# Deferring the opening group's element-wise tail behind the first head, and raising the priority of the meta products

## The chip, the cores and the metric

The kernel runs on one core of one Trainium2 chip. The metric is the device time of one execution in microseconds (us). The engines are PE (TensorE, matrix products), DVE (VectorE) and POOL (GpSimd) for element-wise work, ACT (ScalarE) for copies and activations, and SP (SyncE), which issues all DMAs from one queue in order. Each engine runs its own list of instructions strictly in order.

## The reference

One decoder layer on a sequence of 2048 rows with 16 learned meta rows put in front. The combined projection gives eight parts of 512 columns; four feed a gated short convolution, four a retention.

```python
hn = rms_norm(h, norm_g)
proj = jnp.einsum('bld,de->ble', hn, w_in)
cx, cb, cc, cg, q, k, v, rg = jnp.split(proj, N_PROJ, axis=-1)
conv_out = short_conv_branch(cx, cb, cc, conv_w) * jax.nn.silu(cg)   # cb * conv(cc * cx)
...
ret_out = ret.astype(h.dtype) * jax.nn.silu(rg)
mixed = jnp.concatenate([conv_out, ret_out], axis=-1)
return h + jnp.einsum('ble,ed->bld', mixed, w_out)
```

All of it is in float32. The retention works in chunks of 128 rows with a state per head; a final norm follows.

## The kernel before, in words

Every large product is made of three matmuls: each operand is split into a high part (`mh`, `wh`: a copy to the fp32r format on ACT) and a low part (`ml`, `wl`: source minus high part on DVE, L113), and high x low, low x high and high x high are summed in one PSUM bank. `split` (L98) does this.

The sequence is worked in two blocks of 1024 rows (r = 0, 1), each in two halves of 512 (j = 0, 1). In a block come eight units: four convolution groups and four retention heads. In block 0 the order is group 4 (the "opening group"), heads 0 to 3, then groups 5, 6 and 7 (`UNITS`, L36). Each unit has two "quads". A quad multiplies a 2 x 2 arrangement of weight blocks by a 2 x 2 arrangement of activation blocks. `quad` (L201) does this in seven products (a Winograd form) of 12 matmuls each; their operands are sums and differences of blocks. The weight sums are made in place on POOL by `stationary` (L123), from four raw tiles `ra` and a sum tile `sa`; their parts `wh`, `wl` have three buffers each. The third product needs a difference formed on POOL, its cast on ACT, its `wl` on DVE, and also the copy `tc` (L217) of the bank that the first product filled, since it goes on summing in that bank. `quad_plain` (L249) does the same quad without sums in eight products, 96 matmuls; the opening group uses it because the activation sums are not ready yet. The parts `ml` for two of the sums (`late_parts`, L791) take over buffers that the opening group's second quad still reads.

What each quad leaves in PSUM is taken over by a function `take`. For the opening group the first quad gives `u` (the product of two projections, copied by ACT and multiplied by DVE), which is multiplied by the row factors `rr2`, gets two columns in front by `carry` (L446, three small copies on POOL, the first two values coming from the meta rows through `meta_carry`, L424) and goes through three convolution taps, `taps` (L452: one on ACT, two on DVE for each half). The second quad gives for each half a gate and another factor: `take_plain` (L506) copies the bank to `cb` on ACT, multiplies the gate by `rr` on DVE, applies Silu on ACT, multiplies the tap result `c` by `rr` on POOL, and multiplies `c` by each of the two on DVE. `store_mixed` (L439) writes `c` to memory.

`meta_products` (L388) multiplies a unit's raw weight blocks by the 16 normalized meta rows: 16 small matmuls (32 passes on PE, plain float32) into one bank, then four small ACT copies to `mk`. `ahead` (L744) calls it for the next unit at the end of each unit. POOL may overwrite the raw blocks only after these matmuls.

The tile framework schedules all instructions by a priority, in essence the order in which the code writes them, and by its own estimate of when operands are ready; the resulting per-engine lists are fixed at build time. `tc.high_priority(offset=HIGH)` lets instructions be given out as if they were written 400 places earlier. `HIGH` is already defined in the kernel before (L30).

Of the kernel before, what the change touches and what calls it, by code (L numbers as in the profile page):

```python
# [14 lines left out]
P = 128  # L15
# [55 lines left out]
def hybrid_trunk(ctx: ExitStack, tc: tile.TileContext, t, out: bass.AP, chunk_decay):  # L71
# [20 lines left out]
    def gen(name="g"):  # L92
        return sb.tile([P, HB + 16], F32, name=name, tag="g", bufs=GEN)[:, : 2 + HB]
# [155 lines left out]
    def quad_plain(w, m, take, middle=None):  # L249

        for j in range(2):
            banks = [ps_proj() for _ in range(2)]
            for half in range(2):
                for kt in range(KH):
                    ks = slice(kt * P, (kt + 1) * P)
                    mh, ml = m[BLOCK[half][j]][kt]
                    for i in range(2):
                        wh, wl = w[2 * i + half]
                        for n, (a, b) in enumerate(((wl, mh), (wh, ml), (wh, mh))):
                            nc.tensor.matmul(  # L260
                                banks[i], a[:, ks], b, start=half + kt + n == 0,
                                stop=half == 1 and kt == KH - 1 and n == 2,
                            )
# [124 lines left out]
    def meta_products(blocks):  # L388

        bank = ps_misc()  # L390
        four = [bank[i * 32 : i * 32 + NMETA, :P] for i in range(4)]
        for kt in range(KH):
            for i in (3, 2, 1, 0):
                nc.tensor.matmul(  # L394
                    four[i], meta_s[:, i % 2 * KH + kt, :], blocks[i][:, kt * P : (kt + 1) * P],
                    start=kt == 0, stop=kt == KH - 1,
                )
        scratch = sb.tile([P, HB], F32, name="mk", tag="tc", bufs=COPIES).rearrange("p (a c) -> p a c", a=CH)
        for i in range(4):
            nc.scalar.copy(out=scratch[:NMETA, i], in_=four[i])  # L400
        return scratch
# [56 lines left out]
            )  # L458
        return c

    def conv_group(g, r, m, f, blocks, ahead, first=(), between=()):


        between = iter(between)
        u = [gen("u") for _ in range(2)]
        rr, rr2 = ([a[:, j * HB : (j + 1) * HB] for j in range(2)] for a in f[:2])
        held = [None]

        def mul(eng, out, a, b):
            eng.tensor_tensor(out=out, in0=a, in1=b, op=ALU.mult)  # L470

        def take(i, j, pp, c):
            s = u[j][:, 2:]
            if c is None:
                mul(nc.vector, s, pp, s)
            elif i == 1:
                add(nc.vector, c, pp, c)
                held[0] = c
            else:
                add(nc.vector, s, pp, c)  # L480
                mul(nc.vector, s, s, rr2[j])
                if j == 1:
                    mul(nc.gpsimd, s, s, held[0])

        def take_plain(i, j, pp, c):
            s = u[j][:, 2:]
            if i == 0:
                nc.scalar.copy(out=s, in_=pp)
            else:
                mul(nc.vector, s, pp, s)  # L490

        blocks, meta = blocks
        if len(first) > 0:
            quad_plain(first[0], m, take_plain)
        else:
            quad(stationary(blocks), m, take)
        next(between, lambda: None)()
        if len(first) > 0:
            for j in range(2):
                mul(nc.vector, u[j][:, 2:], u[j][:, 2:], rr2[j])  # L500
# [5 lines left out]
        def take_plain(i, j, pp, c):  # L506
            c = gen("cb")[:, :HB]
            nc.scalar.copy(out=c, in_=pp)
            if i == 0:
# [19 lines left out]
        if len(first) > 1:  # L529
            quad_plain(first[1], m, take_plain)  # L530
        else:
            quad(stationary(load_raw(w_loads(n))), m, take)
        next(between, lambda: None)()
        blocks = ahead()
        for j in range(2):
            store_mixed(r, j, g, cs[j])
        return blocks
# [216 lines left out]
    for r in range(NR):  # L754
        f = factors[r]
        rot_t = sb.tile([P, 2, BLK], F32, name="rot_t", tag="rot_t", bufs=1)
        p0 = NMETA + r * BLK

        def load_tables():
            nc.sync.dma_start(rot_t, t["rot"][:, :, p0 : p0 + BLK])  # L760

        if r == 0:
            w = [None] * 4
            loads = w_loads(2 * NG)

# [30 lines left out]
            between = (lambda: None, late_parts)  # L796
# [10 lines left out]
        units = UNITS[r]  # L807
        for n, unit in enumerate(units):
            following = units[n + 1] if n + 1 < len(units) else None
            rest = lambda: ahead(r, following)  # L810
            special = (first, between) if n == 0 else ()
            if unit < NG:
                blocks = head(unit, r, m, rot_t, f, blocks, rest, *special)
                if unit > 0:
                    next(later, None)
                    next(later, None)
            else:
                blocks = conv_group(unit - NG, r, m, f, blocks, rest, *special)
                if n > 0:
                    for _ in range(4 - r):  # L820
                        next(steps, None)

    m, b = moving(load_w_out)
    final_g = row_tile("final_g")
# [41 lines left out]
```

## Time and profile before

| | us |
|---|---|
| time, median of 3 runs (lowest, highest) | 907.0 (906.9, 907.28) |
| the profiled execution's own time | 906.71 |
| its span, first to last instruction | 904.9 |
| TensorE busy | 882.2 |
| VectorE busy | 717.7 |
| ScalarE busy | 407.7 |
| GpSimd busy | 392.2 |

A matmul's row in the timeline shows a duration of about 0.39 us, but successive matmuls overlap: the step from start to start is what it costs. "Idle before" in square brackets names what ended an engine's wait. All times in rows count from the span's start. Line numbers are those of the kernel before unless a sentence says otherwise.

### The profile page before, as it was taken

To read this page: it belongs to the slowest core of one execution; us is meant where nothing else is said; L and a number is where in the kernel's file an instruction comes from. 1 tells how busy PE (TensorE), PEld (TensorE's weight loads), DVE (VectorE), ACT (ScalarE), POOL (GpSimd) and SP (SyncE) were. 2 spreads that over 40 slices of the span, in tenths; PEclk is the share of its full clock that TensorE was granted. 3 is DMA by queue.
4 is the path that set the end of the run, shared out by engine and by line. 5 is a ranking of instruction groups with operands and counts; after the bars stand their busy time and mean duration, and the time that the engine had idled before them with its cause. 6 is when DMAs were issued, how large, how long until landed. Compare 5 with 4: busy or idle time off the path is not lost.

```text
span 904.9 us, 12864 instructions
## 1 busy us (share of the span) xinstructions
PE 882.2 (97%) x4407; PEld 726.5 (80%) x4407; DVE 717.7 (79%) x1176; ACT 407.7 (45%) x816; POOL 392.2 (43%) x291
## 2 busy tenths in 40 slices
PE   8988999999999999999999999999999999999996
PEld 5767788888888787788888888888887878788885
DVE  6897788898867966899889899777667697876664
ACT  8772433434244454655333332433333474555553
POOL 0552231313333565351333323345546444777773
PEclk9998999999999999999999999999999999999999
DMA  9712115436234252754125272113221685555532
GB/s 331 233 37 73 45 48 164 140 81 211 60 95 139 72 161 71 248 193 140 35 74 199 77 234 70 51 55 93 54 87 48 208 277 174 166 181 157 184 122 80
DMA packets 76242, 116.94 MB, mean 129 GB/s; under 512 B 7632, under 2 KB 24336, under 8 KB 76176
## 3 DMA queue, kind: packets, MB, share of 16 engines
q1 hardware_dynamic: 76176, 116.11, 39.9%
q8 instruction: 35, 0.57, 0.3%
q14 instruction: 31, 0.25, 0.1%
HBM read 90.92 MB, written 25.17 MB: 128 GB/s over the span
## 4 chain that ended last, share of the span: by engine, by line
PE 81%; DVE 8%; DMA 3%; ACT 3%; issue 2%; POOL 1%; SPq 0%; POOLq 0%; DVEq 0%; ACTq 0%
PE pj L210 67%; PE pj L260 5%; DVE ml L113 2%; DVE wl L113 2%; PE ms L642 1%; PE ms L619 1%; PE ms L643 1%; PE ms L632 1%; DMA ra<-in_x 1%; DMA x<-in_xT 1%; PE ms L394 1%; PE ms L604 1%; PE ms L609 1%; PE ms L666 1%; ACT mh L104 1%
## 5 line engine op out<-in xcount | busy, mean ns | idle before, releaser
L210 PE MATMUL pj<-mh,wl 128*128 128x512 f32 x1008 | 400.5, 397 | 9.6 <-DVE wl L113 7.0
L210 PE MATMUL pj<-ml,wh 128*128 128x512 f32 x1008 | 394.7, 392 | 1.1 <-DVE ml L113 1.1
L210 PE MATMUL pj<-mh,wh 128*128 128x512 f32 x1008 | 394.1, 391 | 0.0
L101 ACT CAST wh<-ra 128x512 fp32r<-128x512 f32 x216 | 133.9, 620 | 318.7 <-PE pj L210 275.8
L210 PEld LDWEIGHTS pj<-mh,wl 128*128 128x128 f32 x1008 | 189.9, 188 | 52.2 <-DVE wl L113 7.4
L113 DVE TENSOR_TENSOR wl<-ra,wh 128x512 fp32r<-128x512 f32 x216 | 194.0, 899 | 40.7 <-ACT wh L101 40.2
L210 PEld LDWEIGHTS pj<-mh,wh 128*128 128x128 f32 x1008 | 189.7, 188 | 39.8
L210 PEld LDWEIGHTS pj<-ml,wh 128*128 128x128 f32 x1008 | 190.1, 189 | 39.1 <-DVE ml L113 1.4
L113 POOL TENSOR_TENSOR ra<-ra 128x512 f32<-128x512 f32 x72 | 112.9, 1568 | 87.4 <-DVE qg L587 32.2
L110 POOL TENSOR_TENSOR sa<-ra 128x512 f32<-128x512 f32 x36 | 53.8, 1495 | 124.4 <-DVE wl L113 53.3
L113 POOL TENSOR_TENSOR ra<-sa,ra 128x512 f32<-128x512 f32 x36 | 51.2, 1423 | 92.4 <-DVE wl L113 88.9
L217 ACT COPY tc<-pj 128x512 f32<-128x512 f32 x108 | 62.6, 580 | 0.0
L260 PE MATMUL pj<-mh,ml 128*128 128x512 f32 x128 | 48.7, 397 | 2.2 <-DVE ml L113 1.7
L260 PE MATMUL pj<-ml,mh 128*128 128x512 f32 x128 | 50.3, 393 | 0.1
L260 PE MATMUL pj<-mh,mh 128*128 128x512 f32 x128 | 50.0, 393 | 0.0
L655 POOL TENSOR_TENSOR rp<-rs,neg_half 128x4 f32<-128x4 f32 x16 | 19.9, 1245 | 49.5 <-DVE rs L110 49.3
L470 POOL TENSOR_TENSOR c<-c,rr 128x512 f32<-128x512 f32 x16 | 29.6, 1852 | 25.3 <-DVE c L470 13.5
L696 DVE TENSOR_TENSOR yo<-pj,yo 128x512 f32<-128x512 f32 x32 | 22.0, 688 | 21.2 <-PE pj L210 11.4
L101 ACT CAST wh<-sa 128x512 fp32r<-128x512 f32 x36 | 22.4, 622 | 31.8 <-PE pj L210 31.6
L113 DVE TENSOR_TENSOR ml<-t,mh 128x512 fp32r<-128x512 f32 x40 | 35.6, 936 | 0.8 <-ACT mh L101 0.8
L659 DVE TENSOR_SCALAR pm<-ms,mv,rp 128x128 f32<-128x128 f32 x64 | 21.9, 405 | 15.8 <-POOL rp L655 15.8
L701 POOL TENSOR_TENSOR z<-yo,final_g 128x512 f32<-128x512 f32 x16 | 26.2, 1635 | 18.5 <-DVE yo L696 18.5
(132 smaller groups left out, 1129.2 us busy)
## 6 DMA issues: line engine op xcount, KB each, us to landing
ra<-in_w_in SPq DMA_DIRECT2D x128, 256.0 KB, 2.7
x<-in_xT SPq DMA_DIRECT2D x48, 256.0 KB, 5.0
w<-in_w_out SPq DMA_DIRECT2D x32, 256.0 KB, 5.1
ra<-mixed SPq DMA_DIRECT2D x32, 256.0 KB, 2.7
yo<-in_x SPq DMA_DIRECT2D x32, 256.0 KB, 4.1
ra<-in_x SPq DMA_DIRECT2D x16, 256.0 KB, 3.2
mixed<-c SPq DMA_DIRECT2D x16, 256.0 KB, 2.5
mixed<-qg SPq DMA_DIRECT2D x16, 256.0 KB, 2.3
```

The costliest lines, as they stand in the source:

```text
L101: nc.scalar.copy(out=hi, in_=src)
L104: nc.scalar.mul(hi, src, scale)
L110: eng.tensor_tensor(out=out, in0=a, in1=b, op=ALU.add)
L113: eng.tensor_tensor(out=out, in0=a, in1=b, op=ALU.subtract)
L210: nc.tensor.matmul(bank, a[:, ks], b, start=first and kt == 0 and n == 0, stop=kt == KH - 1 and n == 2, skip_group_check=not first,)
L217: nc.scalar.copy(out=c, in_=bank)
L260: nc.tensor.matmul(banks[i], a[:, ks], b, start=half + kt + n == 0, stop=half == 1 and kt == KH - 1 and n == 2,)
L470: eng.tensor_tensor(out=out, in0=a, in1=b, op=ALU.mult)
L655: nc.gpsimd.tensor_tensor(out=rp, in0=rs, in1=neg_half.rearrange("p (c a) -> p c a", a=1), op=ALU.pow)
L659: nc.vector.tensor_scalar(out=y[:, cs], in0=o[:, cs], scalar1=mv[:, c, 0:1], scalar2=rp[:, c, :], op0=ALU.subtract, op1=ALU.mult,)
L696: last[0] = nc.vector.tensor_tensor(out=y, in0=pp, in1=y, op=ALU.add)
L701: nc.gpsimd.tensor_tensor(out=ys[i][j], in0=y, in1=final_g[:, j * HB : (j + 1) * HB], op=ALU.mult)
```

## The change

`conv_group` loses its special path for the opening group, which gets a function of its own, `group_plain`. It issues both plain quads with takes that only copy: the first quad's `take` is as before, the second's copies all four banks to `cb` tiles and does nothing more. `meta_carry` stands between the quads. The rest (`u` times `rr2`, `carry`, taps, gates, multiplies, stores) is put in a closure, `complete`, which the first head calls between its two quads. `late_parts` and `ahead` keep their place at the end of the opening group. Second, the matmuls of `meta_products` are wrapped in `tc.high_priority`.

```diff
@@ meta_products
+        with tc.high_priority(offset=HIGH):
             for kt in range(KH):
                 for i in (3, 2, 1, 0):
                     nc.tensor.matmul(
                         four[i], meta_s[:, i % 2 * KH + kt, :], blocks[i][:, kt * P : (kt + 1) * P],
...
+    def group_plain(g, m, f, meta, first, between, ahead):
...
+        quad_plain(first[0], m, take)
+        meta_carry(g, meta)
+
+        def take(i, j, pp, c):
+            c = gen("cb")[:, :HB]
+            nc.scalar.copy(out=c, in_=pp)
+            raws.append(c)
+
+        quad_plain(first[1], m, take)
+        between()
+        blocks = ahead()
+
+        def complete():
+            for j in range(2):
+                mul(nc.vector, u[j][:, 2:], u[j][:, 2:], rr2[j])
+            carry(u, g, 0)
+            for j in range(2):
+                gate, other = raws[2 * j : 2 * j + 2]
+                c = taps(u[j], g)
+                mul(nc.vector, gate, gate, rr[j])
+                nc.scalar.activation(gate, gate, AF.Silu)
+                mul(nc.gpsimd, c, c, rr[j])
+                mul(nc.vector, c, c, gate)
+                mul(nc.vector, c, c, other)
+                store_mixed(0, j, g, c)
+
+        return blocks, complete
@@ conv_group
-        def take_plain(i, j, pp, c):
-            c = gen("cb")[:, :HB]
-            nc.scalar.copy(out=c, in_=pp)
-            if i == 0:
-                mul(nc.vector, c, c, rr[j])
-                nc.scalar.activation(c, c, AF.Silu)
-                mul(nc.gpsimd, cs[j], cs[j], rr[j])
-            mul(nc.vector, cs[j], cs[j], c)
@@ the loop over units
+            if r + n == 0:
+                blocks, complete = group_plain(unit - NG, m, f, blocks[1], first, late_parts, rest)
+                special = (), (complete,)
+            elif unit < NG:
+                blocks = head(unit, r, m, rot_t, f, blocks, rest, *(special if unit == 0 else ()))
```

What the scheduler makes of it is shown at three places. In the rows, `x2` or `x16` counts like instructions in a row.

The first place is the turn from the opening group to the first head, on DVE. The rows run from the carry copy (`carry<-ms`) to the `wl` of the first head's third product; `c`, `cb` and `u` belong to the opening group, `ml` to the activation sums, `mk` to the meta products. Before:

```order
L430 COPY carry_78<-ms 128x2
L456 SCALAR_TENSOR_TENSOR c<-u,conv_w,c 128x512
L470 TENSOR_TENSOR u<-u,rr_363 128x512
L456 SCALAR_TENSOR_TENSOR c<-u,conv_w,c 128x512 x2
L470 TENSOR_TENSOR cb<-cb,rr 128x512
...
L110 TENSOR_TENSOR mk<-mk 16x128
L470 TENSOR_TENSOR c<-c,cb 128x512 x3
L113 TENSOR_TENSOR wl<-ra,wh 128x512
```

And now (L431 is the carry copy there):

```order
L470 TENSOR_TENSOR cb<-cb,rr 128x512
...
L431 COPY carry_78<-ms 128x2
L470 TENSOR_TENSOR u<-u,rr_363 128x512
L110 TENSOR_TENSOR mk<-mk 16x128 x2
L470 TENSOR_TENSOR cb<-cb,rr 128x512
L113 TENSOR_TENSOR ml_672<-t_307,mh_671 128x512
L113 TENSOR_TENSOR wl<-ra,wh 128x512
```

All taps and all multiplies into `c` have left this stretch, and the gate's multiply of the first half has moved ahead of the carry copy. The same place on ACT, from the second half's row factors (`rr`, `rr_363`) to the copy `tc` of the head's first bank, before:

```order
L295 ACTIVATE rr_363<-ms 128x512
L454 ACTIVATE c<-u,conv_w 128x512
L508 COPY cb<-pj 128x512 x3
L101 CAST mh_694<-t_307 128x512
L508 COPY cb<-pj 128x512
...
L511 ACTIVATE cb<-cb 128x512
L217 COPY tc<-pj 128x512
L101 CAST wh<-ra 128x512
L101 CAST wh<-sa 128x512
```

And now:

```order
L295 ACTIVATE rr_363<-ms 128x512
L401 COPY mk<-ms 16x128 x4
L484 COPY cb<-pj 128x512
L101 CAST mh_671<-t_307 128x512
L101 CAST wh<-ra 128x512
L484 COPY cb<-pj 128x512
L101 CAST mh_679<-t_309 128x512
L499 ACTIVATE cb<-cb 128x512
L101 CAST wh<-sa 128x512
L217 COPY tc<-pj 128x512
```

The two other `cb` copies (first half) now stand before the casts of `t`, earlier than these rows. The cast of the third product's weights moved ahead of the copy `tc`. On POOL the first difference `ra<-ra` now stands behind the two small copies into `u` and ahead of the small copy back to the carry; the multiply of `c` by `rr` that stood ahead of it went behind the differences of the second quad.

The second place is the first head's second quad on DVE, from the end of the first quad's rotation (`kv<-kv,rot`) on. Now there stand:

```order
L110 TENSOR_TENSOR kv<-kv,rot 128x512
L457 SCALAR_TENSOR_TENSOR c<-u,conv_w,c 128x512 x3
L113 TENSOR_TENSOR wl<-ra,wh 128x512
L457 SCALAR_TENSOR_TENSOR c<-u,conv_w,c 128x512
L113 TENSOR_TENSOR wl<-sa,wh 128x512
L470 TENSOR_TENSOR c<-c,cb 128x512
L110 TENSOR_TENSOR qg<-pj,tc 128x512
L113 TENSOR_TENSOR wl<-ra,wh 128x512
L470 TENSOR_TENSOR c<-c,cb 128x512 x2
```

Before, the same rows stood there without those that write `c`. The tail of the opening group has moved here; the first `wl` of these rows belongs to the third product of the second quad, and the last multiply into `c` stands two rotation rows further down, right ahead of the `wl` that follows.

The third place is PE at the end of the opening group: `L290` spreads row factors, `L429` (now `L430`) transposes the meta row, `L394` (now `L395`) are the meta products of head 0. In the difference of the lists:

```order
 L290 MATMUL ms<-rot,ones 128x512
-L429 MATMUL ms<-ident,mk 128x16
+L430 MATMUL ms<-ident,mk 128x16
+L395 MATMUL ms<-ra,meta_s 16x128 x16
 L260 MATMUL pj<-mh_240,mh_298 128x512
...
 L260 MATMUL pj<-mh_252,mh_298 128x512
-L394 MATMUL ms<-ra,meta_s 16x128 x16
 L210 MATMUL pj<-mh_115,wl 128x512
```

The 16 products moved up by 13 matmuls, right behind the transpose. The later ones, which before stood in two or three pieces with 12 matmuls between (8 + 8, three times 6 + 10, 8 + 7 + 1, 5 + 11), now stand as 16 in one piece, where the first piece stood; only head 0's 8 + 8 stands where the second piece was. On SP the two stores of the opening group's `c` stand behind 13 weight loads where it was 7, and right ahead of the load of `mr`, the meta keys' rotation table.

More of the change, by code (lines that the diff above doesn't have):

```diff
@@ L391, in meta_products @@
         four = [bank[i * 32 : i * 32 + NMETA, :P] for i in range(4)]
[L392 to L397, printed above, removed]
+        with tc.high_priority(offset=HIGH):
+            for kt in range(KH):
+                for i in (3, 2, 1, 0):
+                    nc.tensor.matmul(
+                        four[i], meta_s[:, i % 2 * KH + kt, :], blocks[i][:, kt * P : (kt + 1) * P],
+                        start=kt == 0, stop=kt == KH - 1,
+                    )
         scratch = sb.tile([P, HB], F32, name="mk", tag="tc", bufs=COPIES).rearrange("p (a c) -> p a c", a=CH)
@@ L459, in taps, with mul, take, conv_group @@
         return c
-    def conv_group(g, r, m, f, blocks, ahead, first=(), between=()):
-        between = iter(between)
+    def group_plain(g, m, f, meta, first, between, ahead):
+        u = [gen("u") for _ in range(2)]
+        raws = []
+        rr, rr2 = ([a[:, j * HB : (j + 1) * HB] for j in range(2)] for a in f[:2])
+        def mul(eng, out, a, b):
+            eng.tensor_tensor(out=out, in0=a, in1=b, op=ALU.mult)
+        def take(i, j, pp, c):
+            s = u[j][:, 2:]
+            if i == 0:
+                nc.scalar.copy(out=s, in_=pp)
+            else:
+                mul(nc.vector, s, pp, s)
+        quad_plain(first[0], m, take)
+        meta_carry(g, meta)
+        def take(i, j, pp, c):
+            c = gen("cb")[:, :HB]
[18 more added lines that the diff above has]
+        return blocks, complete
+    def conv_group(g, r, m, f, blocks, ahead):
         u = [gen("u") for _ in range(2)]
@@ L483, in take @@
                     mul(nc.gpsimd, s, s, held[0])
-        def take_plain(i, j, pp, c):
-            s = u[j][:, 2:]
-            if i == 0:
-                nc.scalar.copy(out=s, in_=pp)
-            else:
-                mul(nc.vector, s, pp, s)
-        blocks, meta = blocks
[L493 to L500, printed above, removed]
+        blocks, meta = blocks
+        quad(stationary(blocks), m, take)
         if meta:
@@ L528, in conv_group @@
         n = 2 * (NG + g) + 1
[L529 to L533, printed above, removed]
+        quad(stationary(load_raw(w_loads(n))), m, take)
         blocks = ahead()
@@ L794, in late_parts @@
                         parts(m, i, kt, held[kt])
-            between = (lambda: None, late_parts)
+            between = ()
             later = prepare(load_x(1), sums_x, gain_of)
@@ L807, in hybrid_trunk @@
         units = UNITS[r]
+        special = (first, between)
         for n, unit in enumerate(units):
@@ L817, in hybrid_trunk @@
             else:
[L818 to L821, printed above, removed]
+                blocks = conv_group(unit - NG, r, m, f, blocks, rest)
+                for _ in range(4 - r):
+                    next(steps, None)
     m, b = moving(load_w_out)
```

5 lines of the change are left out of this document (removed).

## Prediction

> **What bounds the kernel now.** I read the page first. TensorE (PE) is busy nearly all the time, so a change pays only where PE stands still, runs at a lower clock, or does extra work.
>
> ```profile
> PE 882.2 (97%) x4407; PEld 726.5 (80%) x4407; DVE 717.7 (79%) x1176; ACT 407.7 (45%) x816; POOL 392.2 (43%) x291
> ```
>
> The second view is the list of PE's waits (us in total, times, longest). Two of its lines lie where this change works.
>
> ```profile
> PE pj L210 <- DVE wl L113: 7.0, 2, 6.5
> PE pj L210 <- ACT cb L508: 0.4, 1, 0.4
> ```
>
> The longest is one wait of 6.5 us on VectorE (DVE) for a `wl`, the low part of a weight tile. PE's timeline (start, duration) puts it in the first head's first quad, ahead of its third product.
>
> ```profile
> 63.57 0.39 PE L210 MATMUL pj<-mh,wh 128*128 128x512 f32 x1
> 70.42 0.80 PE L210 MATMUL pj<-mh,wl 128*128 128x512 f32 x1 [6.46 <-DVE wl L113]
> ...
> 73.58 0.46 PE L210 MATMUL pj<-ml,wh 128*128 128x512 f32 x1
> 73.88 0.40 PE L210 MATMUL pj<-mh,wh 128*128 128x512 f32 x1
> 74.11 0.40 PE L210 MATMUL pj<-mh,wl 128*128 128x512 f32 x1
> ```
>
> After the wait eight matmuls take from 70.42 to 73.88, then the step is 0.23 again. The windows of these two stretches (PE, PEld, DVE, ACT, POOL, then the granted clock) say why: the clock fell during the wait and was 0.54 behind it, while DVE was busy for all of the 6.40 us.
>
> ```profile
> 64.00:70.40 6.40, 0.00 (x0) 0.00 (x0) 6.40 (x10) 1.66 (x3) 2.94 (x2) 0.73 0.04 13
> 70.40:74.00 3.60, 3.58 (x9) 2.86 (x10) 3.52 (x6) 0.00 (x0) 0.38 (x1) 0.54 0.89 246
> ```
>
> So DVE's queue is the cause, and its timeline shows what stood in front of the `wl` at 69.70.
>
> ```profile
> 55.12 0.15 DVE L430 COPY carry<-ms 128x2 f32<-128x2 f32 x1
> 55.55 0.75 DVE L456 SCALAR_TENSOR_TENSOR c<-u,conv_w,c 128x512 f32<-128x512 f32 x1 [0.28 <-POOL u L447]
> 56.21 0.69 DVE L470 TENSOR_TENSOR u<-u,rr 128x512 f32<-128x512 f32 x1
> 56.81 2.72 DVE L456 SCALAR_TENSOR_TENSOR c<-u,conv_w,c 128x512 f32<-128x512 f32 x2
> 59.46 1.78 DVE L470 TENSOR_TENSOR cb<-cb,rr 128x512 f32<-128x512 f32 x1
> 61.16 0.74 DVE L456 SCALAR_TENSOR_TENSOR c<-u,conv_w,c 128x512 f32<-128x512 f32 x1
> 61.82 0.68 DVE L470 TENSOR_TENSOR cb<-cb,rr 128x512 f32<-128x512 f32 x1
> 62.42 3.46 DVE L113 TENSOR_TENSOR ml<-t,mh 128x512 fp32r<-128x512 f32 x2
> ...
> 67.09 0.67 DVE L470 TENSOR_TENSOR c<-c,cb 128x512 f32<-128x512 f32 x1
> ...
> 67.89 1.88 DVE L470 TENSOR_TENSOR c<-c,cb 128x512 f32<-128x512 f32 x3
> 69.70 0.67 DVE L113 TENSOR_TENSOR wl<-ra,wh 128x512 fp32r<-128x512 f32 x1
> ```
>
> **The change part by part.** The sum is made against the profiled execution's own 906.71 us, of which 904.9 are its span; it lies 0.3 below the median of 907.0, so no correction is made.
>
> *1. The tail of the opening group leaves DVE's queue.* Behind the `wl` now go four tap steps (0.75 + 2.72 + 0.74) and four multiplies by the gate and the other bank (0.67 + 1.88): 6.76 us of DVE's time. By the order, between the carry copy and this `wl` remain `u` times `rr2`, two small sums, one `cb` times `rr` and one `ml`. If nothing else is late, the wait of 6.46 goes. With it goes the low clock: eight matmuls in 3.46 us in place of 8 x 0.23 = 1.84, so 1.62.
>
> *2. PE's start on the head.* At the end of the opening group stand the small meta products (32 passes), then a wait of 0.41 for a copy of the first half's banks, which ScalarE (ACT) gave out behind a tap.
>
> ```profile
> 56.38 0.39 PE L260 MATMUL pj<-mh,mh 128*128 128x512 f32 x1
> 56.70 1.07 PE L394 MATMUL ms<-ra,meta_s 128*16 128x128 f32 x32
> 58.18 0.51 PE L210 MATMUL pj<-mh,wl 128*128 128x512 f32 x1 [0.41 <-ACT cb L508]
> 58.52 0.40 PE L210 MATMUL pj<-ml,wh 128*128 128x512 f32 x1
> ```
>
> ACT's two copies of the first half now stand ahead of the casts of `t`, so this wait goes. The meta products go 13 matmuls up, into an interruption that PE has there anyway. From 56.38 to 58.52 are 2.14 us, where two steps would be 0.46: 1.68 for interruption, wait and passes. The passes remain. A pass costs (1.07 - 0.62) / 18 = 0.025 (the 14 passes of the next fence take 0.62), 32 of them 0.80. What goes is 0.88.
>
> *3. The other meta products, now in one piece.* An interruption has a price beside its passes, read where 14 passes stand alone.
>
> ```profile
> 300.78 0.39 PE L210 MATMUL pj<-mh,wh 128*128 128x512 f32 x1
> 301.10 0.62 PE L394 MATMUL ms<-ra,meta_s 128*16 128x128 f32 x14
> 301.65 0.51 PE L210 MATMUL pj<-mh,wl 128*128 128x512 f32 x1
> 302.00 0.40 PE L210 MATMUL pj<-ml,wh 128*128 128x512 f32 x1
> ```
>
> From 300.78 to 302.00 are 1.22; less two steps (0.46) and 14 passes (0.35) leaves 0.41. By the order three interruptions more disappear: one at the end of head 0, two at the end of group 5. At the ends of heads 1 to 3 and of group 6 a 6 + 10 or 5 + 11 becomes 16 with as many interruptions as before: nothing. 3 x 0.41 = 1.23. No block has to land earlier there, since the first piece already read all four blocks.
>
> Without anything new, 906.71 - 6.46 - 1.62 - 0.88 - 1.23 = 896.52.
>
> *4. What is late next at the third product.* Not DVE any more. POOL forms the block differences, and ACT's order is new: `wh<-ra`, copy `cb`, `mh<-t`, Silu, `wh<-sa`, and only then the copy `tc`, on which the third product waits too. Durations:
>
> ```profile
> 55.33 0.18 POOL L447 COPY u<-carry 128x2 f32<-128x2 f32 x1 [3.77 <-DVE carry L430]
> 57.03 0.57 POOL L450 COPY carry<-u 128x2 f32<-128x2 f32 x1 [1.52 <-DVE u L470]
> 58.95 1.74 POOL L113 TENSOR_TENSOR ra<-ra 128x512 f32<-128x512 f32 x1
> 63.63 1.71 POOL L113 TENSOR_TENSOR ra<-sa,ra 128x512 f32<-128x512 f32 x1
> ```
> ```profile
> 58.98 0.64 ACT L101 CAST mh<-t 128x512 fp32r<-128x512 f32 x1
> 59.50 0.61 ACT L508 COPY cb<-pj 128x512 f32<-128x512 f32 x1
> ```
>
> DVE's carry copy ends at 55.27, now one `cb` multiply (0.68) later, 55.95. POOL: 0.18 + 1.74 + 0.57 + 1.71 to 60.15. Then six operations of ACT, each 0.52 from start to start as in the rows and 0.1 for the last one's end, to 63.4; with 0.62 each, to 63.9. PE asks for it at 63.57 + 0.23 - 0.88 = 62.9. A wait of 0.5 to 1.0; I take 0.7. Its bounds: 0, if POOL starts a little earlier, and 2.4, if one more POOL operation's length (1.71) comes in. DVE's `wl` is done at 60.15 + 0.62 + 0.67 = 61.5, before PE's demand.
>
> *5. The tail in its new place.* Three taps stand on DVE right ahead of the `wl` of the second quad's third product.
>
> ```profile
> 88.33 0.69 DVE L113 TENSOR_TENSOR wl<-ra,wh 128x512 fp32r<-128x512 f32 x1
> ```
> ```profile
> 91.15 0.39 PE L210 MATMUL pj<-mh,wl 128*128 128x512 f32 x1
> ```
>
> That `wl` ends at 89.02, 2.13 ahead of its matmul. Three taps of 0.75 are 2.25, at the mean of the slower pair (2.72 / 2 = 1.36) 4.08: PE waits 0.1 to 2.0. I take 0.3, near the undisturbed rows, since POOL's two multiplies by `rr` come only behind the taps. These two stand ahead of POOL's next `sa`, which is for head 1, a whole quad away. On SyncE's queue (SP) the two stores of `c` move behind six more weight loads and stand ahead of the load of `mr`.
>
> ```profile
> 95.78 0.69 DVE L113 TENSOR_TENSOR wl<-ra,wh 128x512 fp32r<-128x512 f32 x1
> ```
> ```profile
> 69.19 0.98 SPq L441 DMA_DIRECT2D mixed<-c  x2
> ...
> 96.88 0.42 SPq L412 DMA_DIRECT2D mr<-in_rot_m  x1
> ```
>
> The loads ahead of the stores can now go as buffers come free instead of after 69.19. By the order the last multiply into `c` stands right ahead of the `wl` that started at 95.78. Nine us earlier that is 86.8, and `mr` was issued at 96.88, which becomes 87.9; so the stores are ready about when `mr` is due, and I give them nothing. If that cover is gone, `mr` is late by as much.
>
> Forecast: 896.52 + 0.7 + 0.3 = **897.5 us**.
>
> [...]
> [...]
>
> **The rivals.**
> *A. DVE and POOL collide at the third product.* DVE's `u` times `rr2` meets POOL's difference, POOL's carry copy waits for it, and the chain of part 4 is longer by one operation of 1.71. For it: the 1.78 and 0.68 above for the same multiply. Against: POOL does fewer multiplies there now. 897.5 + 1.7 = 899.2. Chance 0.17.
> *B. POOL takes DVE's place.* POOL's first difference starts no earlier than its 58.95. Then 58.95 + 1.74 + 0.57 + 1.71 = 62.97, six steps of ACT to 66.2, a wait of 3.3, at which I count the clock's 1.62 as not saved. 896.52 + 3.3 + 1.62 + 0.3 = 901.7. Against: what held POOL there was a tap multiply, which is gone from this place. Chance 0.10.
> *C. The tail comes back as a wait in the second quad.* All of its 6.76 us lands ahead of one `wl` whose margin is 2.13: 4.6 of wait, and the clock's 1.62 again: 896.52 + 0.7 + 4.6 + 1.62 = 903.4. Against: five of the eight operations stand behind the `wl`. Chance 0.05.
> *D. Slower: the stores hold SP.* If the last `c` is late by d, `mr` and the loads behind it are late by d, DVE stands at the rotation of the meta keys with the next `wl` behind it, and PE waits d plus 1.62. It is slower than before from d = 906.71 - 897.5 - 1.6 = 7.6 us; at 10 it gives 909.1. For it: a queue in order. Against: eight DVE operations of 0.7 would need more than twice their time. Chance 0.03.
> *E. No change:* a new wait of about 9 us at any of these places: 906.7. Chance 0.03.
>
> **How the numbers follow.** The forecast has the remaining 0.62. Low end: no leftover wait, 896.5, less 0.1 for each of the four removed interruptions: 896.1. High end: both bounds of parts 4 and 5, 896.52 + 2.4 + 2.0 = 900.9, moved up to 901.5 to take in most of B; C, D, E and the upper part of B stay out, some 0.15. About 0.2% (1.8 us) is what a measurement of this kernel can tell from no change. Faster: forecast, A, B and C, 0.94. Same: E, 0.03. Slower: D, 0.03.
>
> **What would show it.** Right: no PE wait over 3 us between 55 and 100, granted clock 1.00 throughout, a wait of up to 1 us at the third product put down to ACT's `tc` or `wh`, and the first matmul of the head at about 57.4 with no wait. Wrong: a wait on POOL's differences of 3 us (B), on `wl` at the second quad's third product (C), or PE or DVE idle for `mr` (D). If the gap closes and the time falls by less than 6 us, the saving was given back in heads 1 to 3, where I expect no new wait.

## The result and the profile after

The changed kernel takes 896.7 us (median of 4 runs, 896.07 to 897.41) beside 907.0 (906.95; 4 runs, 905.79 to 907.28): ratio 0.9889, 95% interval 0.9872 to 0.9906, about 10 us less. Its profiled execution took 896.51 with a span of 894.7. The first view is the page's busy line; PE's busy time is 3.9 us less, the rest of the gain is idle time that went.

```profile
PE 878.3 (98%) x4407; PEld 726.1 (81%) x4407; DVE 722.4 (81%) x1176; ACT 406.7 (45%) x816; POOL 403.4 (45%) x291
```

PE's waits after the change (us in total, times, longest): the 6.5 for a `wl` is gone. The waits for `pm`, in heads 1 and 2, and for `qg` are new, and so are the 1.0 in the line of `wl` and one of the two 0.7 in the line of `tc`; the other wait of each of these two lines stood there before.

```profile
PE ms L659 <- DVE pm L651: 2.3, 2, 1.2
...
PE pj L210 <- DVE wl L113: 1.5, 2, 1.0
PE pj L210 <- ACT tc L217: 1.3, 2, 0.7
...
PE pj L210 <- DVE qg L110: 0.6, 1, 0.6
```

PE's timeline at the two places of parts 2 and 4: the meta products stand at 52.48 behind the transpose, the first matmul of the head follows with no wait at 56.56 (58.18 before), and the third product starts at 62.83 (70.42 before).

```profile
52.32 0.23 PE L430 MATMUL ms<-ident,mk 16*128 16x16 f32 x1
52.48 1.07 PE L395 MATMUL ms<-ra,meta_s 128*16 128x128 f32 x32
...
56.33 0.39 PE L260 MATMUL pj<-mh,mh 128*128 128x512 f32 x1
56.56 0.39 PE L210 MATMUL pj<-mh,wl 128*128 128x512 f32 x1
...
61.77 0.39 PE L210 MATMUL pj<-mh,wh 128*128 128x512 f32 x1
62.83 0.50 PE L210 MATMUL pj<-mh,wl 128*128 128x512 f32 x1 [0.67 <-ACT tc L217]
```

ACT's timeline in front of it is the chain that part 4 wrote down, in its order and with its step of 0.52; it waits for POOL ahead of its first cast.

```profile
59.63 0.62 ACT L101 CAST wh<-ra 128x512 fp32r<-128x512 f32 x1 [2.45 <-POOL ra L113]
...
61.69 0.60 ACT L101 CAST wh<-sa 128x512 fp32r<-128x512 f32 x1
62.20 0.58 ACT L217 COPY tc<-pj 128x512 f32<-128x512 f32 x1
```

The windows (columns as in the prediction's) show that the clock no longer falls behind this place (1.00), and where the work went: in 74 to 100 DVE is busy for 24.96 of 26.00 us and PE loses 1.54.

```profile
70.40:74.00 3.60, 3.60 (x17) 2.98 (x17) 1.29 (x2) 0.62 (x1) 1.17 (x1) 1.00 0.43 132
74.00:100.00 26.00, 24.46 (x134) 18.84 (x133) 24.96 (x37) 9.13 (x17) 7.07 (x6) 1.00 0.21 62
```

In this stretch PE waits twice in the head's second quad, and not at the third product but later. DVE's timeline shows the tail among the `wl`, and POOL's its two multiplies by `rr`. While POOL multiplies, a tap takes 1.78 and a multiply 1.77; three taps elsewhere take 2.07 together.

```profile
91.64 0.47 PE L210 MATMUL pj<-mh,wl 128*128 128x512 f32 x1 [0.96 <-DVE wl L113]
95.23 0.50 PE L210 MATMUL pj<-mh,wl 128*128 128x512 f32 x1 [0.58 <-DVE qg L110]
```
```profile
79.19 2.07 DVE L457 SCALAR_TENSOR_TENSOR c<-u,conv_w,c 128x512 f32<-128x512 f32 x3
81.17 0.68 DVE L113 TENSOR_TENSOR wl<-ra,wh 128x512 fp32r<-128x512 f32 x1
81.78 1.78 DVE L457 SCALAR_TENSOR_TENSOR c<-u,conv_w,c 128x512 f32<-128x512 f32 x1
83.48 0.68 DVE L113 TENSOR_TENSOR wl<-sa,wh 128x512 fp32r<-128x512 f32 x1
84.08 1.77 DVE L470 TENSOR_TENSOR c<-c,cb 128x512 f32<-128x512 f32 x1
...
90.81 0.68 DVE L113 TENSOR_TENSOR wl<-ra,wh 128x512 fp32r<-128x512 f32 x1
```
```profile
81.33 1.68 POOL L470 TENSOR_TENSOR c<-c,rr 128x512 f32<-128x512 f32 x1 [4.06 <-DVE c L457]
83.63 1.67 POOL L470 TENSOR_TENSOR c<-c,rr 128x512 f32<-128x512 f32 x1 [0.62 <-DVE c L457]
```

Where the time came from is read by comparing the starts of the same large matmul in two traces. Its lead is how much earlier it starts in the changed kernel. The table gives how the lead grows from place to place, for the first pair of traces and for a second pair (both kernels taken once more), beside the forecast.

| from ... to | forecast | first pair | second pair |
|---|---|---|---|
| start to the opening group's middle | 0 | 1.05 | 0.13 |
| ... first matmul of head 0 (part 2) | 0.88 | 0.57 | 0.91 |
| ... its third product (parts 1 and 4) | 6.46 - 0.7 = 5.76 | 5.97 | 6.22 |
| ... behind the low clock (part 1) | 1.62 | 1.55 | 1.94 |
| ... end of head 0 (0.41 of part 3, part 5) | 0.41 - 0.3 = 0.11 | -2.16 | -2.17 |
| ... end of head 3 | 0 | -1.00 | -0.97 |
| ... past groups 5 and 6 (rest of part 3) | 0.82 | 2.10 | 2.11 |
| ... past 692 us | 0 | 1.13 | 1.30 |
| ... end | 0 | 1.02 | 0.03 |
| sum | 9.19 | 10.23 | 9.50 |

The first 1.05 and the last 1.02 are no work of the change, since the second pair lacks them. Of the second pair's 1.30, 0.23 comes at 384 us and the rest at 692.

### The profile page after: what moved, and what is told of

Read it like the earlier page. It is cut to its first block, busy times and chain, and to the rows that moved or that the text cites. A ratio compares the mean times of both kernels' runs of the same rounds, so it can differ in the third digit from the quotient of the medians.

```text
span 894.7 us, 12868 instructions
## 1 busy us (share of the span) xinstructions
PE 878.3 (98%) x4407; PEld 726.1 (81%) x4407; DVE 722.4 (81%) x1176; ACT 406.7 (45%) x816; POOL 403.4 (45%) x291
## 4 chain that ended last, share of the span: by engine, by line
PE 80%; DVE 11%; issue 3%; ACT 2%; DMA 2%; POOL 1%; SPq 0%; POOLq 0%; ACTq 0%; DVEq 0%
PE pj L210 62%; PE pj L260 10%; DVE wl L113 2%; PE ms L659 1%; PE ms L660 1%; PE ms L649 1%; PE ms L636 1%; DVE rot L561 1%; DVE ml L113 1%; PE ms L683 1%; PE ms L395 1%; DVE w L113 1%; PE ms L621 1%; DVE x L174 1%; PE ms L626 1%
## 5 line engine op out<-in xcount | busy, mean ns | idle before, releaser
L113 DVE TENSOR_TENSOR wl<-ra,wh 128x512 fp32r<-128x512 f32 x216 | 191.3, 887 | 36.9 <-ACT wh L101 36.3
L110 POOL TENSOR_TENSOR sa<-ra 128x512 f32<-128x512 f32 x36 | 57.0, 1584 | 118.5 <-DVE wl L113 48.1
L514 POOL TENSOR_TENSOR c<-c,rr 128x512 f32<-128x512 f32 x14 | 26.6, 1900 | 21.3 <-DVE c L457 12.0
L715 ACT ACTIVATE rot<-yo 128x512 f32<-128x512 f32 x32 | 20.2, 630 | 33.1 <-DVE yo L713 32.7
L514 POOL TENSOR_TENSOR c<-c,tc 128x512 f32<-128x512 f32 x14 | 25.9, 1852 | 19.9 <-ACT tc L540 19.8
```

What stands on the lines that cost most here:

```text
L110: eng.tensor_tensor(out=out, in0=a, in1=b, op=ALU.add)
L113: eng.tensor_tensor(out=out, in0=a, in1=b, op=ALU.subtract)
L715: nc.scalar.activation(junk, y, AF.Square, accum_out=ss[:, i, j : j + 1])
```

## The experiments

All times stand beside runs of the kernel before on the same chip (medians 906.4 to 906.9). A kernel that ran once has no interval.

**tail_only: the deferred tail without the priority.** From the changed kernel:

```diff
-        with tc.high_priority(offset=HIGH):
             for kt in range(KH):
```

> The opening group's tail deferred, the meta products at their old priority. Theory T1 (the tail in VectorE's queue held the third product; the priority only saves interruptions of TensorE, 0.41 each, and reorders heads 1 to 3): the wait of 6.46 at the first head's third product shrinks to 1 to 2 us and the granted clock stays at 1.00 there; about 899 us, between the changed kernel (896.7) and 901. Heads 1 and 2 show no wait on pm (the changed kernel has two of 1.2). Rival T2 (GpSimd's block differences, which wait for the meta products, are what the third product needs, so that the priority is the larger part): a wait of over 3 us on a wl or wh remains, the clock falls again, and the time is 902 to 905.

Measured: 897.98 us (897.5 to 899.64), ratio 0.9898 (0.9881 to 0.9914). The lead at the third product is 7.41 and behind the low clock 9.03. PE does not wait at the third product at all, where I expected 1 to 2 us and the changed kernel has 0.67: on ACT the copies `cb`, the casts of `t` and the Silu stand ahead of `wh<-ra` here, and only `wh<-sa` stands between it and `tc`.

```profile
60.67 0.62 ACT L101 CAST wh<-ra 128x512 fp32r<-128x512 f32 x1 [1.21 <-POOL ra L113]
...
61.84 0.59 ACT L217 COPY tc<-pj 128x512 f32<-128x512 f32 x1
```

In heads 1 to 3 the lead stays (6.88, then 6.85), and PE waits for no `pm` there; past groups 5 and 6 it does not grow (6.85). So the tail alone closes the gap, and the leftover wait at the third product, the losses in heads 1 to 3 and the gain of the groups belong to the priority. Beside the tail the priority brings little: the median is 0.7 above that of after_again on the same chip, and the two ranges cannot tell that from nothing.

**prio_only: the priority without the tail.** From the kernel before:

```diff
+        with tc.high_priority(offset=HIGH):
             for kt in range(KH):
```

> The kernel before with the meta products at high priority and nothing else. T1: the wait of about 6.5 us and the fall of the clock stay; only interruptions of TensorE go, less what heads 1 and 2 lose by waits on pm: 904.5 to 906.5 us. T2: the wait falls to under 3 us, and the time to about 900.

Measured: 900.79 (899.76 to 901.39), ratio 0.9929 (0.9915 to 0.9944). I had taken the two edits for separate, and the 6.46 for the tail's alone; that expectation missed, its rival hit. The rows of POOL, DVE and PE show why: with the meta products done at 53.7 the raw blocks may be overwritten, POOL's first difference runs at 54.61 instead of 58.95, and the `wl` of the third product stands at 62.25, ahead of the multiplies into `c` and not behind them. Those now stand in front of the fourth product's `wl`, and the wait comes back there with 2.08.

```profile
54.61 1.29 POOL L113 TENSOR_TENSOR ra<-ra 128x512 f32<-128x512 f32 x1
```
```profile
62.25 0.67 DVE L113 TENSOR_TENSOR wl<-ra,wh 128x512 fp32r<-128x512 f32 x1
...
64.71 1.77 DVE L471 TENSOR_TENSOR c<-c,cb 128x512 f32<-128x512 f32 x1 [1.19 <-POOL c L471]
67.66 0.69 DVE L471 TENSOR_TENSOR c<-c,cb 128x512 f32<-128x512 f32 x1 [1.17 <-ACT wh L101]
68.26 0.68 DVE L113 TENSOR_TENSOR wl<-sa,wh 128x512 fp32r<-128x512 f32 x1
```
```profile
58.47 0.50 PE L210 MATMUL pj<-mh,wl 128*128 128x512 f32 x1 [1.56 <-ACT cb L509]
69.00 0.79 PE L210 MATMUL pj<-mh,wl 128*128 128x512 f32 x1 [2.08 <-DVE wl L113]
```

Alone, the tail brings 8.9 us and the priority 6.1; together they bring 9.7 on this chip (after_again; 10.3 in the first measurement). Both shorten the same wait.

**before_again and after_again: both kernels once more.**

> The kernel before once more, for a second trace. The changed kernel's trace is 1.0 us ahead after the first 20 us and gains 2.1 more between 690 and 740 us, in places whose instructions the change does not move. If this is run variation (T1), this trace differs from the first trace of the same kernel by about 1 us at one of these places; if the change does it by earlier arrival of buffers (T3), both traces of before agree there within 0.2.

> The changed kernel once more, on the chip of the other three: 896 to 897.5 us. T1: waits of 0.7 at the first head's third product, about 1.5 in its second quad and twice 1.2 on pm in heads 1 and 2 stand again at the same instructions, since the order is fixed; the first 20 us and the stretch from 690 to 740 may differ by about 1 us.

Measured: 906.52 in one run, and 897.24 (896.38 to 899.27), ratio 0.9895 (0.9878 to 0.9911). They are the second pair of the table: every step inside the change repeats within 0.4 us. The two traces of the kernel before differ by 0.9 in the opening group, which is run variation, and agree within 0.1 from 690 to 740 us; there the two traces of the changed kernel differ by 1.1, since PE waits 1.16 for an `ml` in one of them alone.

**prio_head0: the priority for head 0's products only, without the tail.** From the kernel before:

```diff
-    def meta_products(blocks):
+    def meta_products(blocks, urgent=False):
...
+        with tc.high_priority(offset=HIGH) if urgent else nullcontext():
...
-            rest = lambda: ahead(r, following)
+            rest = lambda: ahead(r, following, r + n == 0)
```

> The kernel before with high priority for head 0's meta products alone. T1a (the third product's wl stood behind the tail in VectorE's order because GpSimd's first difference had to wait for these 16 products; they alone explain what prio_only gained at the first head): third product within 1 us of prio_only's 64.0 us, a wait of about 2 on the fourth product's wl, the clock low behind it, and a time near 902. Rival T1 as predicted (only the tail's length counts): the third product starts near 70 and the time is about 906.

Measured: 902.46 in one run. The waits at the head's first matmul (1.53) and at the fourth product (2.08) are those of prio_only, and there is no wait for `pm`. So the early difference on POOL comes from head 0's 16 products alone. Beside prio_only it gains 1.0 in heads 1 to 3 and loses 2.1 at the groups.

**prio_groups: the change, with the priority only where a group calls for the next unit's products.** From the changed kernel:

```diff
-        with tc.high_priority(offset=HIGH):
+        with tc.high_priority(offset=HIGH) if urgent else nullcontext():
...
-            rest = lambda: ahead(r, following)
+            rest = lambda: ahead(r, following, unit >= NG)
```

> The changed kernel with the high priority only for meta products given out at the end of a group, not at the end of a head. T1 (the waits on pm in heads 1 and 2 come from the priority there, and cost 1.0 net of the gains beside them): these two waits are gone, group 5's two saved interruptions stay, the time is 1.0 lower than the changed kernel's, about 896.2 on this chip if that stands at 897.2. Rival T2 (the waits come from the tail's shift of the heads): they stay and the time is the same.

Measured: 896.41 (895.63 to 897.38), ratio 0.9886 (0.9869 to 0.9902). PE's waits for `pm` are gone, the lead stays through heads 1 to 3 (6.66, then 6.68), and groups 5 and 6 still give 2.1. The stretch of heads 1 to 3 is thus 1.0 shorter than in the changed kernel; the two medians cannot be told apart, because other places of these runs differ by as much.

**fold_groups: prio_groups, and POOL multiplies the other factor instead of `c`.**

```diff
-                mul(nc.gpsimd, c, c, rr[j])
+                mul(nc.gpsimd, other, other, rr[j])
```

`other` is ready in the first quad, so POOL's two multiplies leave the second quad; DVE's work is the same.

> As prio_groups, and the tail's two GpSimd multiplies by rr go to the second factor instead of c, so that they no longer wait for the taps and run before head 0's second quad. T-collide (the second quad's loss of 2.0 us is VectorE held up by these two operations: tap 1.78 and multiply 1.77 beside 0.75 and 0.67): the loss falls to under 0.7, the time to about 894.7. T-load (the loss is the 6.8 us of moved VectorE work itself): the loss stays over 1.4 and the time within 0.6 of prio_groups.

Measured: 895.93 (895.22 to 896.75), ratio 0.988 (0.9865 to 0.9895), 0.5 below prio_groups, which the two ranges cannot tell apart. By the time alone that is what a pure load on DVE would give. The trace says otherwise: from behind the third product to the end of head 0 the lead changes by +0.2 (7.39, then 7.59), where the changed kernel loses 2.16 and prio_groups 2.2, and no wait of PE is left there. DVE is about as full as in the changed kernel (24.37 of the 26.00 us from 74 to 100), so its load alone is not what PE waits for. DVE's rows for the same instructions:

```profile
82.93 0.69 DVE L113 TENSOR_TENSOR wl<-ra,wh 128x512 fp32r<-128x512 f32 x1
83.53 0.75 DVE L457 SCALAR_TENSOR_TENSOR c<-u,conv_w,c 128x512 f32<-128x512 f32 x1
84.19 0.69 DVE L113 TENSOR_TENSOR wl<-sa,wh 128x512 fp32r<-128x512 f32 x1
84.79 1.29 DVE L470 TENSOR_TENSOR c<-c,cb 128x512 f32<-128x512 f32 x2
```

The tap that took 1.78 takes 0.75 and the multiply that took 1.77 about 0.64: 2.2 us, the size of the loss. The gain does not show in the time because this execution started head 0 later than prio_groups did (lead 0.38, not 1.67) and lost 1.2 in the output stage, where its clock fell (below).

So the excess of 1.03 and 1.13 in these two rows of the changed kernel is there beside POOL's multiplies of 1.68 and 1.67, and gone without them. By what means one engine holds up the other was not shown.

**delay5 and delay9: a longer wait at the third product.** The changed kernel with n copies of a raw block onto itself on DVE, ahead of the cast for that product (n = 5, 9):

```diff
+        for _ in range(delay):
+            nc.vector.tensor_copy(out=a11, in_=a11)
...
-            quad(stationary(blocks[0]), m, take)
+            quad(stationary(blocks[0], n if r + h == 0 else 0), m, take)
```

> The changed kernel with five more VectorE copies in place ahead of the cast for the first head's third product (values unchanged), which should make TensorE wait there about 2 us instead of 0.7. [...] T-short (a wait of about 2 is enough, as prio_only's wait of 2.08 suggests): some eight matmuls at steps of 0.43, about 1.6 us more, 899.6.

> The changed kernel with nine copies in place (128x512) on DVE ahead of the cast for the first head's third product, where delay5 had five; nothing computed is changed. The last six stand back to back, and three more DVE operations come ahead of the wl, so that the wait, 2.12 in delay5, should be 4 to 4.6. The question is the clock. In delay5 a wait of 2.12 was followed by clock 1.00; in the kernel before with only the priority a wait of 2.08 was followed by eight matmuls at 0.43 a step. [...]

Measured: 900.39 and 904.53, one run each. In delay5 the wait is 2.12 and the clock behind it 1.00, so the slow matmuls of T-short did not come; the time is near its 899.6, but for another reason: 1.1 was lost to a wait for an `ml` at 727 us and 1.3 at the clock in the output stage. In delay9 the wait is 5.23, longer than I meant, and the clock falls to 0.50 for 6.80 us (65.50 to 72.30); in the 3.40 us ahead of that (62.10 to 65.50) PE was busy for 0.27.

Shorter waits can have a half clock behind them too: in prio_head0 (wait of 2.08, ended at 68.91) and in fold_groups in the output stage, where two waits of 0.58 and 1.11 follow each other. In the 3.40 us ahead of it PE was busy for 1.32 and 1.78, so it was not idle throughout.

```profile
66.70:70.10 3.40, 1.32 (x6) 1.02 (x6) 2.54 (x4) 1.10 (x2) 1.99 (x2) 1.00 0.30 77
70.10:73.50 3.40, 3.40 (x10) 2.54 (x9) 3.37 (x4) 0.12 (x1) 2.12 (x2) 0.51 0.53 154
```
```profile
761.70:765.10 3.40, 1.78 (x7) 1.24 (x8) 3.40 (x5) 1.06 (x3) 1.38 (x1) 0.98 0.27 93
765.10:768.50 3.40, 3.40 (x10) 2.65 (x9) 2.25 (x4) 1.12 (x3) 1.07 (x1) 0.51 0.38 113
```

In prio_head0 the slow stretch begins 1.2 us after the wait is over. The length of a wait alone does not tell what the clock does: 2.08 was followed by 0.51 here and by 0.52 in prio_only (over 3.40 us each), 2.12 in delay5 by 1.00.

From 5.45 us on the granted clock of the kernel before is full for 61.44 us, then half for 6.83 (66.89 to 73.72), then full for 829.44: 18, 2 and 243 times 3.413. The one stretch at full clock in the changed kernel lasts 884.05 us (from 8.12 on), 259 times 3.413. What sets these lengths was not shown, nor how idle PE must be for the clock to fall: with PE busy for 1.57 of 3.40 us (delay5, 61.10 to 64.50) it was 1.00 in the next 3.40, with 1.78 (fold_groups above) it was 0.51.

**tc_first, carry_after and carry_dve: the leftover wait at the third product.** tc_first is fold_groups with the copy `tc` one place earlier on ACT; carry_after is the changed kernel, and carry_dve is fold_groups, with the opening group's three carry copies on DVE instead of POOL:

```diff
-        c = copy(xb)
+        with tc.high_priority(offset=soon) if soon else nullcontext():
+            c = copy(xb)
```

```diff
-            carry(u, g, 0)
+            carry(u, g, 0, nc.vector)
```

> fold_groups with one instruction moved: on ACT the copy tc of the first head's first bank stands ahead of the cast wh<-sa instead of behind it. The cast took 0.52 from start to start, and the matmul waited 1.20 for tc. T-pool and T-act both say the wait falls by that one step, to about 0.7 (tc would start at 63.45 instead of 63.95), and no more, because the operations ahead of tc still stand behind wh<-ra, which waits for POOL; the wl of the fourth product becomes 0.5 later and has room for it. Time 0.5 below fold_groups, about 895.4, which one look cannot tell; the wait can. If the wait does not fall, or one of the same size comes up at the fourth product, ACT's order was not what was late.

> The changed kernel with only the opening group's three carry copies moved from POOL to DVE; the tail and the priority as in the change. It shows what part of the leftover wait at the third product belongs to POOL's order without the other edits. T-pool: POOL's differences at about 53.6 and 55 instead of 55.61 and 58.31, the wait of 0.67 at the third product gone, about 896.0 and the waits in the second quad (0.96 and 0.58) up by as much as PE now comes earlier, since DVE is full there: then the time moves by 0.3 or less. T-act: the wait of 0.5 or more stays at the third product.

> fold_groups with one thing more: the three small carry copies of the opening group (128x2) go from POOL to DVE, so that POOL's list at the first head holds only the three block differences, with nothing ahead of them that waits for the meta row. Theory T-pool: the leftover wait at the third product (1.20 us in fold_groups, put down to ACT's copy tc) begins on POOL: its first difference stands behind the copy that waits 4.37 us for the carry, and its second behind a copy of 1.45, so the cast wh<-ra waits 2.97 for POOL and everything behind it on ACT is late. Without them the differences follow the meta products (end 54.75): 1.35 and 1.29, ready at about 57.5, the cast at about 57.8 instead of 61.39, tc right behind the first product, and the wait at the third product is 0.0 to 0.2: about 1.1 less than fold_groups, 894.8. Theory T-act: it is ACT's own number of operations ahead of tc that makes it late, so the wait stays at 0.5 or more and the time within 0.5 of fold_groups, 895.4 to 896.4. Both: granted clock 1.00 at this place, no wait over 0.6 in the first head's second quad.

Measured: tc_first 894.36 and carry_after 895.72, one run each; carry_dve 893.47 (892.82 to 893.89), ratio 0.9852 (0.9836 to 0.9869). In tc_first the wait is 0.73 instead of 1.20, the step of one cast, as both theories had it. In carry_dve and carry_after no wait is left at the third product. POOL and ACT in fold_groups, and then in carry_dve:

```profile
56.82 0.58 POOL L448 COPY u<-carry 128x2 f32<-128x2 f32 x1 [4.37 <-DVE carry L431]
57.37 1.35 POOL L113 TENSOR_TENSOR ra<-ra 128x512 f32<-128x512 f32 x1
58.66 1.45 POOL L451 COPY carry<-u 128x2 f32<-128x2 f32 x1
60.07 1.29 POOL L113 TENSOR_TENSOR ra<-sa,ra 128x512 f32<-128x512 f32 x1
```
```profile
61.39 0.62 ACT L101 CAST wh<-ra 128x512 fp32r<-128x512 f32 x1 [2.97 <-POOL ra L113]
```
```profile
54.78 3.04 POOL L113 TENSOR_TENSOR ra<-ra 128x512 f32<-128x512 f32 x1 [3.62 <-PE ms L395]
57.90 1.70 POOL L113 TENSOR_TENSOR ra<-sa,ra 128x512 f32<-128x512 f32 x1
```
```profile
59.62 0.62 ACT L101 CAST wh<-ra 128x512 fp32r<-128x512 f32 x1 [1.34 <-POOL ra L113]
```

The first difference starts 2.6 us earlier, right behind the meta products. It also takes 3.04 instead of 1.35, beside the end of a row of six `ml` on DVE, so that the cast comes at 59.62 and not at the 57.8 that I expected; enough is left. The late chain began on POOL: two copies of 128x2, one of which waited for the carry. ACT's order is the other half of it, since tail_only has the same copies on POOL and no wait. In carry_after the lead over the changed kernel is 0.6 at the third product and 0.7 to 0.9 from there on. I had expected the waits in its second quad to grow by what PE comes earlier, so that the time would move by 0.3 or less; they stand at 0.96 and 0.43 (0.96 and 0.58 in the changed kernel), and the gain is kept.

carry_dve is the version that beats both kernels: 12.9 us below the kernel before on the same chip, and 3.2 below the first median of the changed one, with intervals of the two ratios that do not meet.

## Why the prediction was right, and where its steps were not

The time came out 0.8 us below the forecast of 897.5. The large terms held, and two errors of about 3 us in all (part 5 and heads 1 to 3) were made good by gains that I had not counted. That they cancel is luck: 1.3 are the priority's at groups 5 and 6, but 1.1 came at 692 us, where the prediction has no term, and 2.1 of the first pair are no work of the change.

*1 and 4, the wait and what is late next.* Shown. Forecast 5.76 net, measured 5.97 and 6.22; the leftover wait was 0.67 (0.41 in after_again) where I took 0.7, on the engine and the instruction named. That POOL's carry copies stand at the start of the chain, as part 4 reckoned, is shown by carry_after and carry_dve. What the step did not see is that the priority alone would have taken two thirds of the wait (prio_only): the terms of parts 1 and 2 are not separate. Nor did it see that the leftover wait comes with the priority: tail_only has none.

*The clock.* 1.62 forecast, 1.55 and 1.94 measured. The term is right in kind, and its size is chance. In the first trace of the kernel before the half clock lasts 6.83 us, from 66.89 on, and begins during the wait; PE is busy for 3.30 us of it, and half of these is lost. Rival B counts the 1.62 as not saved at a wait of 3.3. No run shows the term at a wait of that length: behind waits of 2.08 the clock was 0.51 and 0.52, behind 2.12 it was 1.00, and behind delay9's 5.23 it was 0.50.

*2, PE's start.* 0.88 forecast, 0.57 and 0.91 measured; that the second agrees is luck. The two traces of the changed kernel agree there, and what differs is the wait of the kernel before, 0.41 and then 0.75. This wait goes with the tail: tail_only gains 0.48 over the first trace here, with the products in their old place. Moving the products was mis-sized: it saves about 0.2, where the forecast has 0.88 - 0.41 = 0.47. Between the two large matmuls around them the step grows from 1.34 to 2.34, so the 32 passes cost 1.00 there and not 0.80.

*3, the interruptions in one piece.* The term was mis-sized. At groups 5 and 6, 0.82 forecast, 2.10 measured; tail_only gains nothing there, so all of it is the priority's. 0.9 of it comes at one matmul of group 6, where the kernel before stands for a transpose and waits, which I had not looked for:

```profile
314.21 0.47 PE L210 MATMUL pj<-mh,wl 128*128 128x512 f32 x1 [0.64 <-ACT wh L101]
```

Its `wh` stands behind a block difference on POOL, which may come earlier when the products have read the blocks earlier. That mechanism is argued from prio_only's rows and was not tried here. The interruptions at the end of group 5 gave 0.5 of the 0.82. The rest is that a 6 + 10 or 5 + 11 in one piece does save: 0.5 for each of heads 1 to 3 and 0.7 for group 6, where I counted nothing because other small matmuls stand there anyway. At the end of head 0 the products stand in one piece in tail_only too, so that interruption goes with the tail and not with the priority.

*5, the tail's new place.* This step failed. I took 0.3 and gave 0.1 to 2.0 for taps ahead of the third product's `wl`; head 0 lost 2.16 although a merged interruption saved there. There was no wait at the second quad's third product at all. The error is in the sentence that POOL's multiplies come only behind the taps: they come behind the first half's taps and beside the second half's, and stretch two DVE operations by 2.2 in a stretch where DVE was full (24.96 of 26.00). fold_groups shows it by taking away just these, with DVE as full as there. It was the mechanism of rival A, which I had looked for at the first quad, 25 us earlier.

*Heads 1 to 3.* "No new wait" was wrong. PE waits twice for `pm` (1.2 each), which the 0.5 saved at each of three heads covers in part: 1.0 lost. prio_groups and tail_only, without priority there, have neither waits nor loss. Why the priority makes `pm` late was not followed.

```profile
168.81 0.49 PE L659 MATMUL ms<-kv,pm 128*128 128x128 f32 x2 [1.18 <-DVE pm L651]
```

*The stores (rival D).* DVE's wait for `mr`, in the kernel before and now, shows that the stores cost nothing.

```profile
99.26 0.35 DVE L417 TENSOR_TENSOR mk<-mk,mr 16x64 f32<-16x64 f32 x2 [1.13 <-DMA mr<-in_rot_m]
```
```profile
94.02 0.35 DVE L418 TENSOR_TENSOR mk<-mk,mr 16x64 f32<-16x64 f32 x2 [0.72 <-DMA mr<-in_rot_m]
```

*Left open.* A wait of 0.75 at 692 us, for a `tc` in block 1, is in both traces of the kernel before and in none of the others, which gives all of them about 1 us. By the rows it is a collision of DVE and POOL once more: in the kernel before a `wl` starts on DVE at 686.98, 0.07 behind POOL's `sa`, and takes 1.76; in the changed kernel the same `wl` starts at 678.54, 0.20 ahead of that `sa`, and takes 0.79. Why its cast on ACT comes 0.3 earlier there was not tried.

## What to carry to other kernels

A deferred tail is not free because its engine has gaps in the new place: put its operations beside what the other engines do there, and count those of DVE that will run beside POOL's element-wise work at the slow length measured for them (1.78 for 0.75 here). Where two edits touch the same wait, run each alone before adding their gains. And when a large wait closes, follow the next one to its first instruction: here two copies of two columns on POOL, with the new order of ACT behind them, held 0.7 to 1.2 us of PE.

## What the runs showed of the hardware

A half-clock stretch of about 3.4 us followed a wait of 2.08 in one piece (prio_only, 0.52; prio_head0, 0.51, where it began 1.2 us after PE was back at work), and waits of 0.58 and 1.11 close together (fold_groups, 0.51). The same pair of waits in the output stage (0.56 to 0.59, then 1.11 to 1.13) stands in seven traces beside that one. In prio_head0, delay5 and delay9 matmuls behind it go at steps of 0.43 us; in the kernel before, prio_groups, after_again and carry_after they stay at 0.23. Whether part of the spread between executions is this was not shown.

POOL's difference of 128x512, 1.28 us at its shortest (changed kernel), took 3.04 beside DVE's back-to-back subtractions (carry_dve), and its multiply by `rr` took 5.67 in prio_only:

```profile
59.01 5.67 POOL L471 TENSOR_TENSOR c<-c,rr 128x512 f32<-128x512 f32 x1
```
